# HGRN2 pair products: level 0 and the diagonal by elementwise products and a matrix of ones

## The chip, the cores and the metric

The kernel runs on one core of one Trainium2 chip. The metric is the device time of one execution in microseconds (us). The kernel before took 3584.81 us (median of 3 runs, 3584.51 to 3585.55).

## The reference, cut to what matters

The model is a two-layer backbone over 1024 latent tokens and 256 context tokens of width 1024. Layer 0 (neighbourhood attention beside mLSTM heads) is not touched. Layer 1 has 16 bidirectional HGRN2 heads with 128 keys (k) and 128 values (v). For each head and direction, with `f` the decay after its sigmoid and lower bound, `b` the running sum of `log f`, and `k = 1 - f`, the reference computes in chunks

```python
o = einsum('bhtk,bhkv->bhtv', qc * exp(b), S)
pair = exp(where(tri, b[t] - b[s], -inf))              # t, s in the chunk, for each k
a = einsum('bhtk,bhtsk->bhts', qc, pair * kc)
o = o + einsum('bhts,bhsv->bhtv', a, vc)
S = exp(bL) * S + einsum('bhsk,bhsv->bhkv', kc * exp(bL - b), vc)
```

and adds the outputs of the two directions. `a[t, s]` is a sum over k of a query, a key and the decays between them. Its diagonal is `q[t]·k[t]` without a decay; the entry of a token with its direct neighbour has one decay factor.

## The kernel before, in words

**Layer 1.** `build` loops over 16 heads. For a head, `hg_proj` multiplies the normalised tokens by 128-column slices of the weights: the decay of both directions (`F`, two halves of 512 tokens, and `Fc` for the context) and the query `q` (two halves, half 1 first). `hg_intra` builds the 128x128 score blocks `A` of 8 chunks (4 in each half). `hg_vz` projects values and the output gate, one context tile and then 8 tiles of 128 tokens with 24 matmuls each (`mm<-hh,wzh` and its fellows for the context, `mm<-wzh,hh` for the 8). `hg_ctx` makes the context state, and `hg_scan` runs the states through the 8 chunks (c = 0 to 7), multiplies by `v`, normalises, gates (`gyn`), transposes and stores. `hg_proj` of the next head follows in the program.

**Precision.** A float32 matrix that goes through a projection is split into two float32r parts: `split` (lines 69 to 72) copies the high part on ScalarE (L71) and subtracts it on VectorE (L72). `dense` (L117, L118, L119) then does three float32r matmuls. The matmuls of `hg_level` (L880), the diagonal (L909) and the scan (L920, L932 to L937) are float32. In the profile each float32 128x128 matmul is two MATMUL records and each float32r matmul one; both are labelled f32.

**`hg_intra`, line 834.** For each half: `K = 1 - F` for both directions, `Q = q * F` for both. Then 7 levels, in each of which half 1 goes before half 0. Level `lev` handles the pairs of tokens that first share a block of `2h = 2^(lev+1)` tokens. `hg_level` (line 866) has ScalarE copy the keys of the level to `gksel` (L875), TensorE multiply them by the queries, four 128x128 blocks to a PSUM tile `s` (L880), and VectorE move the entries of this level to `A`: at level 0 by a multiplication with a float32 mask (L886), later by a predicated copy with a byte mask (L890). VectorE then multiplies four half-size slices of K and Q in place by decays (L898) and shrinks the decay products `gT` (L900). At level 0, L888 adds the two directions' keys into another `gksel`; after level 0 `hg_diag` multiplies these by `q` (L909) and L910 writes the diagonal of `A` by a predicated copy.

**What sets the order.** The program is written for the Tile framework with its own scheduler. It orders the instructions of each engine from its own estimate and puts in the semaphores; then each engine goes through its list. The projections of a head and of the next one fill TensorE between the steps of `hg_intra` and `hg_scan`. Buffers that matter here: `gksel` 3, `gsg` 1 (also the sigmoid of `q` in `hg_proj`, L778, read by L779), PSUM `s` 3 and `mm` 2, `gz` 1 (the gate of a head: written by L800, multiplied by L801, read by `gyn`, L953), `gQ`, `gK` and `gA` 2 each, that is one head's two halves. An `mm` tile of `hg_vz` is free for the next but one when VectorE has done L801.

**The end of a scan half.** After chunk 3 and after chunk 7, ScalarE squares four blocks (L948), GpSimd takes the inverse root (L142, L144), VectorE makes four `gyn` (L953), and TensorE transposes them (L956).

Of the kernel before, what the change touches and what calls it, by code (L numbers as in the profile page):

```python
# [18 lines left out]
P = 128  # L19
# [24 lines left out]
class Prog:  # L44
# [789 lines left out]
    def hg_intra(self, st, pool):  # L834
        nc = self.nc
        n = 512
        hv = {}
        for hf in (1, 0):
            F, q = st["F"][hf], st["q"][hf]
            K = self.t(pool, [P, 2, n], F32, "gK", 2)  # L840
            nc.vector.tensor_scalar(out=K, in0=F, scalar1=-1.0, scalar2=1.0, op0=ALU.mult, op1=ALU.add)
            Q = self.t(pool, [P, 2, n], F32, "gQ", 2)
            for d in range(2):
                nc.vector.tensor_tensor(out=Q[:, 1 - d, :], in0=q, in1=F[:, d, :], op=ALU.mult)
            A = self.t(pool, [P, 4, P], F32, "gA", 2)
            hv[hf] = dict(Q=Q, A=A, T=F, K=K)
        for lev in range(7):
            for hf in (1, 0):
                self.hg_level(hv[hf], lev, pool)
            if lev == 0:  # L850
                for hf in (1, 0):
                    self.hg_diag(hv[hf], st["q"][hf], pool)
        for hf in (1, 0):
            H = hv[hf]
            H["kn"] = []
            for d in range(2):
                p = self.ps("tr", [P, 4, P])
                for c in range(4):
                    nc.tensor.transpose(p[:, c, :], H["K"][:, d, c * P : (c + 1) * P], self.ident)
                k_ = self.t(pool, [P, 4, P], F32, "gkn", 4)  # L860
                nc.scalar.copy(k_, p)
                H["kn"].append(k_)
        return hv


    def hg_level(self, H, lev, pool):
        nc = self.nc
        n, h = 512, 1 << lev
        nb = n // (2 * h)
# [6 lines left out]
        qp = pick(Q)  # L876
        pa = self.ps("s", [P, 4, P])
        nbc = P // (2 * h)
        for c in range(4):
            nc.tensor.matmul(  # L880
                pa[:, c, :].rearrange("p (b s i) -> p b s i", s=2, i=h),
                lhsT=ksel[:, c * P : (c + 1) * P], rhs=qp[:, c * nbc : (c + 1) * nbc], start=True, stop=True,
            )
        if lev == 0:

            nc.vector.tensor_tensor(out=A, in0=pa, in1=self.lmask0.unsqueeze(1).to_broadcast([P, 4, P]), op=ALU.mult)  # L886
            H["ks"] = self.t(pool, [P, n], F32, "gksel", 3)
            nc.vector.tensor_tensor(out=H["ks"], in0=K[:, 0, :], in1=K[:, 1, :], op=ALU.add)  # L888
        else:
            nc.vector.copy_predicated(A, self.lmask[:, lev - 1, :].unsqueeze(1).to_broadcast([P, 4, P]), pa)  # L890
        Tv = Tt.rearrange("p d (b s) -> p d b s", s=2)
        bc = lambda t: t.unsqueeze(2).to_broadcast([P, nb, h])
        Kv, Qv = sel(K), sel(Q)
        for t, i, s, tot in (
            (Kv, 0, 0, Tv[:, 0, :, 1]), (Kv, 1, 1, Tv[:, 1, :, 0]),
            (Qv, 0, 0, Tv[:, 1, :, 1]), (Qv, 1, 1, Tv[:, 0, :, 0]),
        ):
            nc.vector.tensor_tensor(out=t[:, i, :, s, :], in0=t[:, i, :, s, :], in1=bc(tot), op=ALU.mult)  # L898
# [5 lines left out]
    def hg_diag(self, H, q, pool):  # L904
        nc = self.nc
        pa = self.ps("s", [P, 4, P])
        for c in range(4):
            s = slice(c * P, (c + 1) * P)
            nc.tensor.matmul(pa[:, c, :], lhsT=H["ks"][:, s], rhs=q[:, s], start=True, stop=True)  # L909
        nc.vector.copy_predicated(H["A"], self.ident8.unsqueeze(1).to_broadcast([P, 4, P]), pa)  # L910

    def hg_scan(self, h, st, halves, S, pool, y):
        nc = self.nc
# [48 lines left out]
    def build(self):  # L962
        tc, nc, a = self.tc, self.nc, self.a
        dma = nc.sync.dma_start
        with ExitStack() as es:
# [19 lines left out]
            def load(name, shape, eng=nc.gpsimd):  # L985
# [12 lines left out]
                out=self.qkn, in0=qkn[:, 0:1], scalar1=qkn[:, 1:2], scalar2=0.125, op0=ALU.mult, op1=ALU.mult  # L998
# [14 lines left out]
            for i in range(2):  # L1013
# [6 lines left out]
                out=self.lb[:, 1, :], in0=self.lb[:, 0, :], scalar1=-1.0, scalar2=1.0, op0=ALU.mult, op1=ALU.add  # L1020
# [74 lines left out]
            lk = l1.enter_context(tc.tile_pool(name="hgk", bufs=1))  # L1095
            with tc.tile_pool(name="op0", bufs=2) as op, ExitStack() as wl:
                self.gate_bc(0, op, 2, 1)
                later = []
                w1 = self.wo_half(wl, a["woab"], 0, "left", yp, later)
                for tt in [8, 9, 3, 4, 2, 5, 1, 6, 0, 7]:  # L1100
                    xt = self.t(op, [P, D], F32, "ox", 2)[:, 512:D]
                    self.out_tile(w2, 1, tt, self.yd, self.xin(tt), xt, yp, op, 2, part=acc[:, tt, :])
                    nc.gpsimd.dma_start(out=self.x1[tt * P : (tt + 1) * P, 512:D], in_=xt)
                    for ld in later[:2]:
                        ld()
                    later = later[2:]
# [5 lines left out]
                nc.vector.tensor_copy(self.ident8, self.ident)  # L1112
                lm = self.t(op, [P, D], F32, "nx", 1)[:, 0 : 7 * P].rearrange("p (l f) -> p l f", f=P)
                dma(out=lm, in_=a["glm"])
                nc.vector.tensor_copy(self.lmask, lm[:, 1:7, :])
                nc.vector.tensor_copy(self.lmask0, lm[:, 0, :])
                self.gate_bc(0, op, 2, 0)
                wr.close()
                right = es.enter_context(ExitStack())
                self.open_h(right)  # L1120
                self.wp = right.enter_context(tc.tile_pool(name="w1", bufs=2, side="right"))
                self.rawp = op
                self.slabs = 4
                wf = self.wring([a["wc"][:, 2048 : 2048 + P]], P)
                for tt in [8, 9, 4, 5, 6, 7, 0, 1, 2, 3]:
                    xt = self.t(op, [P, D], F32, "ox", 2)
                    dma(out=xt[:, 512:D], in_=self.x1[tt * P : (tt + 1) * P, 512:D])
                    self.out_tile(w1, 0, tt, self.yd, self.xin(tt), xt[:, 0:512], op, op, 2)
                    if tt < 8:
                        nc.gpsimd.dma_start(out=self.x1[tt * P : (tt + 1) * P, 0:512], in_=xt[:, 0:512])  # L1130
                    xn = self.t(op, [P, D], F32, "nx", 1)
                    self.norm(xn, xt, op)
                    self.mod_tr(1, [xn], tt, op, self.h_sink(tt * P, P))

            with l1:
                pool = l1.enter_context(tc.tile_pool(name="hg", bufs=2))
                self.rawp = pool
                l1.enter_context(self.pp.phase(s=3, acc=1))
                st = self.hg_proj(0, pool, wf)
                for h in range(16):  # L1140
                    hv = self.hg_intra(st, pool)
# [3 lines left out]
                    if h < 15:  # L1145
                        st = self.hg_proj(h + 1, pool)
# [163 lines left out]
```

## Time and profile before

| what | value |
|---|---|
| median of 3 runs | 3584.81 us |
| the profiled execution, its own time | 3583.22 us |
| span from its first to its last instruction | 3581.4 us |
| mean granted TensorE clock | 0.992 |
| VectorE, ScalarE, GpSimd busy | 2216.1, 1418.4, 454.6 us |
| HGRN2 heads, first to last `gA` mask product | 1948.7 to 3335.4 us |

The busy share of an engine is an average over stages. A line of the timeline has the start, the time from start to end of the merged instructions, the engine, the source line, the operation with its tiles, the count, and in brackets the engine's idle time just before it with what ended it. On TensorE and VectorE one instruction starts before the one ahead of it has quite ended, so a chain's cost is read from start to start. All times are those of the profiled execution.

### The profile page before, as it was taken

The numbers are of one execution on the slowest core, as the hardware profiler recorded it, in microseconds if no ns is written. First come the engines' busy times: TensorE is split into PE (matmuls) and PEld (weight loads), VectorE is DVE, ScalarE is ACT, GpSimd is POOL, SyncE is SP. The second block draws the span as 40 slices with busy tenths as digits, with TensorE's granted clock in tenths as the row PEclk, the third lists the DMA queues.
The fourth block names the chain that finished last, engine by engine and source line by source line (L and its number), as shares of the span: only waits on it lengthen the run. The fifth ranks groups of instructions, "written<-read, shape, count | busy, mean of one in ns | idle before, by whom it ended". The sixth has DMA issues, their size and how long they took to land.

```text
span 3581.4 us, 65599 instructions
## 1 busy us (share of the span) xinstructions
PE 3516.8 (98%) x24954; PEld 3222.6 (90%) x24954; DVE 2216.1 (62%) x5976; ACT 1418.4 (40%) x3493; POOL 454.6 (13%) x752
## 2 busy tenths in 40 slices
PE   8999999999999999998999999999999999999998
PEld 5879999999999999997788999999999999999877
DVE  4646676666754765664666666666666666666653
ACT  5545555445533434433354333333333333333341
POOL 2222222122211212211010000000000000000000
PEclk9999999999999999999999999999999999999999
DMA  5532323232234434324752111111111111110263
GB/s 206 175 103 75 84 70 84 72 89 75 79 96 148 127 93 141 118 72 141 228 158 62 36 36 36 33 36 36 36 35 34 31 36 36 35 33 27 74 205 116
DMA packets 323051, 305.25 MB, mean 85 GB/s; under 512 B 29016, under 2 KB 280088, under 8 KB 322608
## 3 DMA queue, kind: packets, MB, share of 16 engines
q1 hardware_dynamic: 290704, 217.44, 20.9%
q0 software_dynamic: 32032, 83.61, 6.9%
q8 instruction: 197, 3.23, 0.4%
q14 instruction: 118, 0.97, 0.1%
HBM read 241.49 MB, written 59.30 MB: 84 GB/s over the span
## 4 chain that ended last, share of the span: by engine, by line
PE 88%; issue 5%; DMA 3%; DVE 1%; ACT 1%; POOL 1%; SPq 0%; POOLq 0%; DVEq 0%; ACTq 0%
PE mm L119 18%; PE mm L117 18%; PE mm L118 18%; PE s L880 6%; PE mm L729 2%; PE mm L731 2%; PE mm L730 2%; PE acc L674 2%; PE tr L654 2%; PE acc L458 2%; PE s L467 2%; DMA mld<-md 1%; PE acc L448 1%; PE acc L933 1%; PE s L909 1%
## 5 line engine op out<-in xcount | busy, mean ns | idle before, releaser
L119 PE MATMUL mm<-wh,hl 128*128 128x256 f32 x2560 | 748.9, 293 | 0.2 <-DVE hl L250 0.2
L117 PE MATMUL mm<-wh,hh 128*128 128x256 f32 x2560 | 746.5, 292 | 0.0
L118 PE MATMUL mm<-wl,hh 128*128 128x256 f32 x2560 | 745.4, 291 | 0.0
L119 PEld LDWEIGHTS mm<-wh,hl 128*128 128x128 f32 x2560 | 488.5, 191 | 11.1 <-issue 4.1
L117 PEld LDWEIGHTS mm<-wh,hh 128*128 128x128 f32 x2560 | 488.6, 191 | 7.7 <-issue 1.4
L118 PEld LDWEIGHTS mm<-wl,hh 128*128 128x128 f32 x2560 | 488.7, 191 | 7.1 <-issue 0.8
L117 PE MATMUL mm<-hh,wh 128*128 128x512 f32 (+1 forms) x1216 | 449.5, 370 | 5.9 <-ACT gFc L769 5.9
L118 PE MATMUL mm<-hl,wh 128*128 128x512 f32 (+1 forms) x1216 | 449.2, 369 | 0.0
L119 PE MATMUL mm<-hh,wl 128*128 128x512 f32 (+1 forms) x1216 | 448.7, 369 | 0.0
L119 PE MATMUL mm<-wzh,hl 128*128 128x256 f32 x1024 | 295.3, 288 | 0.0
L117 PE MATMUL mm<-wzh,hh 128*128 128x256 f32 x1024 | 294.2, 287 | 0.0
L118 PE MATMUL mm<-wzl,hh 128*128 128x256 f32 x1024 | 293.9, 287 | 0.0
L875 ACT COPY gksel<-gK 128x512 f32<-128x512 f32 x224 | 148.8, 664 | 317.0 <-PE s L880 159.9
L117 PEld LDWEIGHTS mm<-hh,wh 128*128 128x128 f32 x1216 | 230.3, 189 | 37.5 <-ACT gFc L769 6.2
L119 PEld LDWEIGHTS mm<-hh,wl 128*128 128x128 f32 x1216 | 230.3, 189 | 31.7
L118 PEld LDWEIGHTS mm<-hl,wh 128*128 128x128 f32 x1216 | 230.3, 189 | 30.8
L880 PE MATMUL s<-gQ,gksel 128*128 128x128 f32 x1792 | 254.9, 284 | 0.0
L729 PE MATMUL mm<-woh,yh 128*128 128x512 f32 x576 | 229.8, 400 | 5.6 <-DVE oacc L743 3.5
L880 PEld LDWEIGHTS s<-gQ,gksel 128*128 128x128 f32 x1792 | 231.4, 191 | 1.3
L731 PE MATMUL mm<-woh,yl 128*128 128x512 f32 x576 | 229.6, 399 | 0.8 <-DVE yl L72 0.8
L730 PE MATMUL mm<-wol,yh 128*128 128x512 f32 x576 | 229.3, 398 | 0.4 <-DVE wol L72 0.2
L71 ACT CAST wh<-wraw 128x512 fp32r<-128x512 f32 x240 | 147.2, 619 | 202.8 <-PE mm L118 126.2
(307 smaller groups left out, 7349.6 us busy)
## 6 DMA issues: line engine op xcount, KB each, us to landing
wraw<-yd SPq DMA_DIRECT2D x144, 256.0 KB
wraw<-in_wab_dram SPq DMA_DIRECT2D x112, 256.0 KB
md<-ev POOLq DMA_DIRECT2D x100, 256.0 KB, 2.7
wraw<-in_wc_dram SPq DMA_DIRECT2D x96, 256.0 KB
adar<-in_wada_dram POOLq DMA_DIRECT2D x32, 512.0 KB, 4.8
wraw<-in_wc_dram SPq DMA_DIRECT2D x128, 128.0 KB
adar<-in_wada_dram SPq DMA_DIRECT2D x16, 512.0 KB
wraw<-in_wab_dram SPq DMA_DIRECT2D x64, 128.0 KB
```

The source lines that it names most:

```text
L71: nc.scalar.copy(hi, x)
L117: mm(ps, lhsT=lh(k), rhs=rh(k), start=(k == 0), stop=False)
L118: mm(ps, lhsT=lh(k), rhs=rl(k), start=False, stop=False)
L119: mm(ps, lhsT=ll(k), rhs=rh(k), start=False, stop=(k == nk - 1))
L458: nc.tensor.matmul(num, lhsT=qc[:, j, :], rhs=C[d][:, j, :], start=False, stop=(j == 1))
L467: nc.tensor.matmul(u, lhsT=st["k"][c][:, j * P : (j + 1) * P], rhs=vw, start=True, stop=True)
L654: nc.tensor.transpose(pt[:nk, i, :], pr[:, o : o + nk], self.ident)
L729: mm(ps, lhsT=yh[:, k, :], rhs=w.h(kk), start=(kk == 0), stop=False)
L730: mm(ps, lhsT=yh[:, k, :], rhs=w.l(kk), start=False, stop=False)
L731: mm(ps, lhsT=yl[:, k, :], rhs=w.h(kk), start=False, stop=(kk == 8 * len(qs) - 1))
L875: nc.scalar.copy(ksel.rearrange("p (b s i) -> p b s i", s=2, i=h), pick(K))
L880: nc.tensor.matmul(pa[:, c, :].rearrange("p (b s i) -> p b s i", s=2, i=h), lhsT=ksel[:, c * P : (c + 1) * P], rhs=qp[:, c * nbc : (c + 1) ...
```

## The change

Level 0 (a token with its pair neighbour) and the diagonal (a token with itself) no longer go through 128x128 matmuls of keys by queries. A new function `hg_near` runs for both halves before the levels. For each of the two cases it has VectorE multiply keys and queries elementwise into a `gsg` tile `pr` of 128 keys by 512 tokens, splits `pr` into float32r parts (two `gksel` tiles), and has TensorE sum over the 128 keys by two matmuls of a 128x128 matrix of ones with 512 columns. Every row of the result then has the sums, and VectorE keeps the entries wanted: the neighbour by a multiplication with the byte mask of level 0, the diagonal by the predicated copy as before. Level 0 of `hg_level` keeps only the decay multiplications. The float32 mask `lmask0` goes, the byte mask grows by one level, and the ones are built once.

```diff
@@ hg_intra
+        for hf in (1, 0):
+            self.hg_near(hv[hf], st["q"][hf], pool)
         for lev in range(7):
             for hf in (1, 0):
                 self.hg_level(hv[hf], lev, pool)
-            if lev == 0:
-                for hf in (1, 0):
-                    self.hg_diag(hv[hf], st["q"][hf], pool)
@@ hg_level
-        ksel = self.t(pool, [P, n], F32, "gksel", 3)
-        nc.scalar.copy(ksel.rearrange("p (b s i) -> p b s i", s=2, i=h), pick(K))
...
-        if lev == 0:
-
-            nc.vector.tensor_tensor(out=A, in0=pa, in1=self.lmask0.unsqueeze(1).to_broadcast([P, 4, P]), op=ALU.mult)
-            H["ks"] = self.t(pool, [P, n], F32, "gksel", 3)
-            nc.vector.tensor_tensor(out=H["ks"], in0=K[:, 0, :], in1=K[:, 1, :], op=ALU.add)
-        else:
-            nc.vector.copy_predicated(A, self.lmask[:, lev - 1, :].unsqueeze(1).to_broadcast([P, 4, P]), pa)
+        if lev > 0:
+            ksel = self.t(pool, [P, n], F32, "gksel", 3)
+            nc.scalar.copy(ksel.rearrange("p (b s i) -> p b s i", s=2, i=h), pick(K))
...
+            nc.vector.copy_predicated(A, self.lmask[:, lev, :].unsqueeze(1).to_broadcast([P, 4, P]), pa)
@@ hg_diag goes, hg_near comes
-        for c in range(4):
-            s = slice(c * P, (c + 1) * P)
-            nc.tensor.matmul(pa[:, c, :], lhsT=H["ks"][:, s], rhs=q[:, s], start=True, stop=True)
-        nc.vector.copy_predicated(H["A"], self.ident8.unsqueeze(1).to_broadcast([P, 4, P]), pa)
+    def hg_near(self, H, q, pool):
+        nc = self.nc
+        n = 512
+        K, Q, A = H["K"], H["Q"], H["A"]
+
+        kx = bass.AP(K.tensor, K[:, 1, 1:n].offset, [list(K.ap[0]), [2, n // 2], [-(n + 1), 2]])
+        qx = bass.AP(Q.tensor, Q.offset, [list(Q.ap[0]), [2, n // 2], [n + 1, 2]])
+        for i in range(2):
+            hi = self.t(pool, [P, n], F32R, "gksel", 3)
+            lo = self.t(pool, [P, n], F32R, "gksel", 3)
+            pr = self.t(pool, [P, n], F32, "gsg", 1)
+            if i == 0:
+                nc.vector.tensor_tensor(out=pr.rearrange("p (b s) -> p b s", s=2), in0=kx, in1=qx, op=ALU.mult)
+            else:
+                nc.vector.tensor_tensor(out=pr, in0=K[:, 0, :], in1=K[:, 1, :], op=ALU.add)
+                nc.vector.tensor_tensor(out=pr, in0=pr, in1=q, op=ALU.mult)
+            self.split(hi, lo, pr)
+            pa = self.ps("s", [P, 4, P])
+            p2 = pa.rearrange("p a b -> p (a b)")
+            nc.tensor.matmul(p2, lhsT=self.ones, rhs=hi, start=True, stop=False)
+            nc.tensor.matmul(p2, lhsT=self.ones, rhs=lo, start=False, stop=True)
+            if i == 0:
+                nc.vector.tensor_tensor(out=A, in0=pa, in1=self.lmask[:, 0, :].unsqueeze(1).to_broadcast([P, 4, P]), op=ALU.mult)
+            else:
+                nc.vector.copy_predicated(A, self.ident8.unsqueeze(1).to_broadcast([P, 4, P]), pa)
@@ build
-                self.lmask = self.t(lk, [P, 6, P], U8, "glm8", 1)
-                self.lmask0 = self.t(lk, [P, P], F32, "glm0", 1)
+                self.lmask = self.t(lk, [P, 7, P], U8, "glm8", 1)
...
+                self.ones = self.t(lk, [P, P], F32R, "ones", 1)
+                nc.vector.tensor_scalar(
+                    out=self.ones, in0=self.ident, scalar1=0.0, scalar2=1.0, op0=ALU.mult, op1=ALU.add
+                )
...
-                nc.vector.tensor_copy(self.lmask, lm[:, 1:7, :])
-                nc.vector.tensor_copy(self.lmask0, lm[:, 0, :])
+                nc.vector.tensor_copy(self.lmask, lm)
```

More of the change, by code (lines that the diff above doesn't have):

```diff
@@ L873, in hg_level @@
         pick = lambda t: _skew(t[:, 0, :].rearrange("p (b s i) -> p b s i", s=2, i=h), 2, n)
-        ksel = self.t(pool, [P, n], F32, "gksel", 3)
-        nc.scalar.copy(ksel.rearrange("p (b s i) -> p b s i", s=2, i=h), pick(K))
-        qp = pick(Q)
-        pa = self.ps("s", [P, 4, P])
-        nbc = P // (2 * h)
-        for c in range(4):
[L880 to L883, printed above, removed]
-        if lev == 0:
-            nc.vector.tensor_tensor(out=A, in0=pa, in1=self.lmask0.unsqueeze(1).to_broadcast([P, 4, P]), op=ALU.mult)
-            H["ks"] = self.t(pool, [P, n], F32, "gksel", 3)
-            nc.vector.tensor_tensor(out=H["ks"], in0=K[:, 0, :], in1=K[:, 1, :], op=ALU.add)
-        else:
-            nc.vector.copy_predicated(A, self.lmask[:, lev - 1, :].unsqueeze(1).to_broadcast([P, 4, P]), pa)
+        if lev > 0:
+            ksel = self.t(pool, [P, n], F32, "gksel", 3)
+            nc.scalar.copy(ksel.rearrange("p (b s i) -> p b s i", s=2, i=h), pick(K))
+            qp = pick(Q)
+            pa = self.ps("s", [P, 4, P])
+            nbc = P // (2 * h)
+            for c in range(4):
+                nc.tensor.matmul(
+                    pa[:, c, :].rearrange("p (b s i) -> p b s i", s=2, i=h),
+                    lhsT=ksel[:, c * P : (c + 1) * P], rhs=qp[:, c * nbc : (c + 1) * nbc], start=True, stop=True,
+                )
+            nc.vector.copy_predicated(A, self.lmask[:, lev, :].unsqueeze(1).to_broadcast([P, 4, P]), pa)
         Tv = Tt.rearrange("p d (b s) -> p d b s", s=2)
@@ L901, in hg_level @@
         H["T"] = Tn
-    def hg_diag(self, H, q, pool):
+    def hg_near(self, H, q, pool):
         nc = self.nc
-        pa = self.ps("s", [P, 4, P])
-        for c in range(4):
-            s = slice(c * P, (c + 1) * P)
-            nc.tensor.matmul(pa[:, c, :], lhsT=H["ks"][:, s], rhs=q[:, s], start=True, stop=True)
-        nc.vector.copy_predicated(H["A"], self.ident8.unsqueeze(1).to_broadcast([P, 4, P]), pa)
+        n = 512
[12 more added lines that the diff above has]
+            self.split(hi, lo, pr)
+            pa = self.ps("s", [P, 4, P])
+            p2 = pa.rearrange("p a b -> p (a b)")
[5 more added lines that the diff above has]
+                nc.vector.copy_predicated(A, self.ident8.unsqueeze(1).to_broadcast([P, 4, P]), pa)
     def hg_scan(self, h, st, halves, S, pool, y):
@@ L1108, in build @@
                 nc.vector.memset(self.zero, 0.0)
-                self.lmask = self.t(lk, [P, 6, P], U8, "glm8", 1)
-                self.lmask0 = self.t(lk, [P, P], F32, "glm0", 1)
+                self.lmask = self.t(lk, [P, 7, P], U8, "glm8", 1)
                 self.ident8 = self.t(lk, [P, P], U8, "ident8", 1)
                 nc.vector.tensor_copy(self.ident8, self.ident)
+                self.ones = self.t(lk, [P, P], F32R, "ones", 1)
+                nc.vector.tensor_scalar(
+                    out=self.ones, in0=self.ident, scalar1=0.0, scalar2=1.0, op0=ALU.mult, op1=ALU.add
+                )
                 lm = self.t(op, [P, D], F32, "nx", 1)[:, 0 : 7 * P].rearrange("p (l f) -> p l f", f=P)
                 dma(out=lm, in_=a["glm"])
-                nc.vector.tensor_copy(self.lmask, lm[:, 1:7, :])
-                nc.vector.tensor_copy(self.lmask0, lm[:, 0, :])
+                nc.vector.tensor_copy(self.lmask, lm)
                 self.gate_bc(0, op, 2, 0)
```

## The prediction

> **What bounds the kernel now.** I read the page first, then busy time by stage, then the timelines of the engines in one head. The page's first lines, and the windows of two heads one after the other (length, then busy time and instructions of TensorE, weight load, VectorE, ScalarE, GpSimd, then the clock):
>
> ```profile
> span 3581.4 us, 65599 instructions
> PE 3516.8 (98%) x24954; PEld 3222.6 (90%) x24954; DVE 2216.1 (62%) x5976; ACT 1418.4 (40%) x3493; POOL 454.6 (13%) x752
> 2592.90:2685.10 92.20, 92.20 (x652) 86.08 (x651) 60.36 (x150) 29.95 (x74) 4.27 (x6) 1.00 0.12 35
> 2685.10:2777.30 92.20, 92.20 (x652) 86.07 (x651) 60.19 (x150) 29.74 (x74) 4.27 (x6) 1.00 0.12 35
> ```
>
> The same counts in windows of 92.20 us: a head takes 92.2 us. TensorE never shows idle at the full clock, VectorE is busy 65%. A modelled end can hide a gap, so I go by starts. TensorE around the end of a head's query projection:
>
> ```profile
> 2682.15 0.39 PE L117 MATMUL mm<-hh,wh 128*128 128x512 f32 x1
> 2682.38 0.39 PE L118 MATMUL mm<-hl,wh 128*128 128x512 f32 x1
> 2682.84 1.16 PE L880 MATMUL s<-gQ,gksel 128*128 128x128 f32 x6
> 2683.83 0.39 PE L934 MATMUL acc<-gS,gQ 128*128 128x128 f32 x2
> 2684.06 0.39 PE L932 MATMUL acc<-gv,gA 128*128 128x128 f32 x2
> 2684.51 0.39 PE L934 MATMUL acc<-gS,gQ 128*128 128x128 f32 x2
> 2691.18 0.61 PE L909 MATMUL s<-gq,gksel 128*128 128x128 f32 x4
> 2691.63 0.38 PE L956 MATMUL tr<-ident,gyn 128*128 128x128 f32 x2
> 2624.03 0.28 PE L117 MATMUL mm<-wzh,hh 128*128 128x256 f32 x1
> 2624.15 0.28 PE L118 MATMUL mm<-wzl,hh 128*128 128x256 f32 x1
> ```
>
> Start to start: a float32r matmul of 512 columns 0.23 us, of 256 columns 0.12 us; a float32 128x128 matmul, two records, 0.225 us (four L909 records in 0.45 us). Level 0 stands out: six L880 records in 0.99 us, so 0.33 us a matmul. Its moving operand alternates between the two directions' queries. So TensorE sets the end of this stage: what leaves it is gained, unless it then has to wait.
>
> **The change part by part.** *TensorE.* Removed in a head: 8 level-0 matmuls x 0.33 = 2.64 us and 8 of the diagonal x 0.225 = 1.80 us. Added: 8 of ones x 0.23 = 1.84 us. That is 2.6 us a head and 41.6 us in 16 heads, without waits. The Trainium skill, page "FP8 and Floating Point Precision", section "TensorE Precision Notes", says that true FP32 takes four passes through the array. By this a 128-column float32 matmul costs as much as one of 512 columns in one pass, at every level; the rows of the diagonal agree (0.225 against 0.23), those of level 0 do not, and by the rule the gain without waits would be 8 x 0.225 x 16, some 29 us.
>
> *VectorE and ScalarE.* A half gains four VectorE instructions of 512 columns: the neighbour product, the product by `q`, and two low parts. (The sum of the keys and the two writes to `A` were there.) ScalarE has two casts in place of one copy. VectorE's price, start to start, stands in this timeline of before around the same place:
>
> ```profile
> 2683.46 0.69 DVE L72 TENSOR_TENSOR wl<-wraw,wh 128x512 fp32r<-128x512 f32 x1 [2.39 <-ACT wh L71]
> 2684.07 0.68 DVE L779 TENSOR_TENSOR gq<-gsg,mm 128x512 f32<-128x512 f32 x1
> 2685.26 0.69 DVE L886 TENSOR_TENSOR gA<-s,glm 128x512 f32<-128x512 f32 x1 [0.51 <-PE s L880]
> 2685.87 0.42 DVE L898 TENSOR_TENSOR gQ<-gQ,gF 128x256 f32<-128x256 f32 x1
> 2688.41 0.61 DVE L953 SCALAR_TENSOR_TENSOR gyn<-acc,gss,gz 128x128 f32<-128x128 f32 x2
> 2688.94 0.75 DVE L898 TENSOR_TENSOR gK<-gK,gF 128x256 f32<-128x256 f32 x2
> 2691.39 0.69 DVE L886 TENSOR_TENSOR gA<-s,glm 128x512 f32<-128x512 f32 x1 [1.70 <-PE s L880]
> 2693.85 0.73 DVE L910 COPY_PREDICATED gA<-ident,s 128x512 f32<-128x512 uint8 x1
> 2694.47 0.41 DVE L815 TENSOR_SCALAR gq<-gFc 128x512 f32<-128x512 f32 x1
> 2694.80 0.75 DVE L898 TENSOR_TENSOR gK<-gK,gT 128x256 f32<-128x256 f32 x2
> 2695.47 0.74 DVE L910 COPY_PREDICATED gA<-ident,s 128x512 f32<-128x512 uint8 x1
> 2696.76 0.28 DVE L801 TENSOR_TENSOR gz<-gz,mm 128x128 f32<-128x128 f32 x1
> 2696.96 0.72 DVE L890 COPY_PREDICATED gA<-glm,s 128x512 f32<-128x512 uint8 x1
> ```
>
> So 0.61 us for 512 columns, 0.62 for a predicated copy, 0.67 for a pair of half-size products, 0.53 for a pair of `gyn`. Eight new instructions are 4.9 us a head. From 2693 on VectorE runs without a gap, so in this stretch it has no room for them. The product reads at a skewed step that no row shows on VectorE: at least the 0.61, at most twice that, by the factor 1.5 of level 0's matmul rounded up; I take 0.61 and keep 1.2 for the range.
>
> *Order.* Each engine goes through its list in order, so I laid the changed kernel's lists beside these prices, with zero at the end of the second query projection (2682.84 in before). In the changed kernel TensorE has the gate and value tiles and the scan of chunks 4 to 7 there; the last scan matmul (chunk 7) stands at 8.2, where before has it at 1.7. The four sums stand at about 7, 10 to 11, 13 and 17, and the third gate tile at 13.45, if nothing waits. That tile needs a PSUM buffer that VectorE's first L801 frees. Behind chunk 7 comes a chain of which before shows each link:
>
> ```profile
> 2684.99 0.28 ACT L948 ACTIVATE gjk<-acc 128x128 f32<-128x128 f32 x1 [1.07 <-PE acc L934]
> 2686.66 0.28 POOL L142 TENSOR_SCALAR gss<-gss 128x4 f32<-128x4 f32 x1 [5.90 <-ACT gjk L948]
> 2687.02 1.36 POOL L144 TENSOR_TENSOR gss<-gss,mhalf 128x4 f32<-128x4 f32 x1
> 2668.55 1.03 POOL L144 TENSOR_TENSOR gss<-gss,mhalf 128x4 f32<-128x4 f32 x1
> 2694.71 0.28 ACT L800 ACTIVATE gz<-mm 128x128 f32<-128x128 f32 x1
> 2699.20 0.27 ACT L799 COPY gv<-mm 128x128 f32<-128x128 f32 x1 [0.39 <-PE mm L119]
> ```
>
> From chunk 7's matmul (2684.51) to `gyn` (2688.41) is 3.9 us; one value copy now stands between the squares (2694.71 less its start, some 0.16 us), so `gyn` starts at 8.2 + 4.1 = 12.3. Behind it in VectorE's list, ahead of L801, the odd heads have two `gyn`, the diagonal's copy, two half-size products, the low part of the third sum, two `gyn`, the sum of the keys and the mask product: 0.53 + 0.62 + 0.67 + 0.61 + 0.53 + 0.61 + 0.61 = 4.2. L801 starts at 16.5 and its 0.28 is over at 16.75; TensorE, there since 13.45, waits 3.3 us. In the even heads the copy and the products stand ahead of `gyn`, 2.9 us remain, L801 is over at 15.5, and the wait is 2.05 us. Both heads run into the low part of the third sum on the way; that wait lies inside these. In before L801 was done at 2697.04, and the second gate tile only ended at 2699.2, so the third had 2 us to spare.
>
> The first four heads and the last have lists of their own. The same steps give 0.5, 6.2 (chunk 7 stands at 13.0 there), 2.0, 2.8 and 2.3 us. With six even heads at 2.05 and five odd at 3.3 the waits are 13.8 + 12.3 + 16.5 = 42.6 us. After the wait the levels are paced by TensorE again: it comes to level 2 about 1 to 2 us after VectorE has the queries ready. Edits that I cost at nothing: ScalarE's casts (ScalarE is busy 30 of 92 us, and the casts are done 1 to 4 us ahead of their matmuls), and ones and masks, built once.
>
> *Sum.* 41.6 less 42.6 us: 1 us slower; where GpSimd's root takes 1.03 and not 1.36 us, as in the other scan half of before, the odd heads have 0.3 us less, 1.6 us in all. I call it nothing: 3583 us, against the 3583.2 us of the profiled execution. The median of the runs lies 1.6 us over that. The Trainium skill, page "SBUF — State Buffer", section "Who interferes with whom", says that a VectorE instruction with two SBUF inputs contends with a GpSimd instruction that reads SBUF. The two lengths of L144 would fit it. By it the even heads, where VectorE is busy during the root, keep 1.36 and the odd ones, where it waits for the root, get 1.03; that is the 1.6 us above.
>
> **The rivals.** *The cover holds* (faster): TensorE has other work or L801 comes sooner, and most of the 41.6 us stays. All of it gives 3541, half of the wait 3562. For it speaks that before has no wait in this stage; against it, that TensorE's list is fixed, and that eight links must all be shorter than their rows. A VectorE chain shorter by 0.5 us gives 8 us, 3575.
>
> *Weight splits ahead of the levels* (slower): in the changed list VectorE's splits of the next head's gate weights stand ahead of the last two levels and of the context's scan (L813, L814). Before has them after:
>
> ```profile
> 2634.46 0.68 DVE L813 TENSOR_TENSOR_SCAN gEc<-gFc,gzero 128x255 f32<-128x255 f32 x1 [1.54 <-issue]
> 2636.42 0.68 DVE L72 TENSOR_TENSOR wzl<-wraw,wzh 128x512 fp32r<-128x512 f32 x1
> 2639.90 0.62 ACT L71 CAST wzh<-wraw 128x512 fp32r<-128x512 f32 x1 [1.50 <-DMA wraw<-in_wc_dram]
> 2640.55 0.69 DVE L72 TENSOR_TENSOR wzl<-wraw,wzh 128x512 fp32r<-128x512 f32 x1 [1.71 <-ACT wzh L71]
> 2644.27 0.62 ACT L71 CAST wzh<-wraw 128x512 fp32r<-128x512 f32 x1 [3.27 <-DMA wraw<-in_wc_dram]
> ```
>
> Each piece waits for a load that starts when the one ahead is split: 2.8 to 3.0 us from split to cast. Three pieces then end about 51.3 in the head, L814 at 52.6, and the context's decay leaves its buffer at 53.1, which TensorE wants at 53.8. It is 0.6 us to spare; beyond it each 1 us of a later load costs 1 us a head. At 1.5 us later it is 0.9 x 16 = 14 us: 3597. A skewed product at 1.2 us costs the even heads up to 0.5 us, 4 us in all.
>
> *The sums are not cheap* (the change does not do what it says): a matmul of ones whose operand was just split starts late. At 0.31 instead of 0.23 each, 128 of them cost 10 us more: 3593.
>
> **How the numbers follow.** A measurement of this kernel can tell about 0.2% from no change, 7 us. The forecast, saving and wait within 7 us of each other, has 0.44; the cover 0.29 (0.10 of it below 3556); the weight splits 0.21; the dear sums 0.06. So faster 0.29, same 0.44, slower 0.27. The likeliest case's own range is 3576 to 3590. The range of 3556 to 3606 takes in waits of up to 1.7 us a head fewer or 1.4 us more than the 2.7 us reckoned, and leaves out 0.1 at each end.
>
> **What would show it.** Right: a steady head of 91 to 93 us; L880 at six sevenths of its count; about 128 ones matmuls at 0.23 us; TensorE idle of 2 to 3 us a head ahead of the third gate tile (L117, `mm<-wzh,hh`) put down to VectorE's `gz`; busy share near 97%. Wrong: a head of 89.6 us and no idle; or idle ahead of L769's tiles, put down to ScalarE (the weight splits), or ahead of the levels' L880; or L144 or the product far from the lengths taken.

## The result, and the profile after

The changed kernel takes 3604.04 us (median of 6 runs, 3600.99 to 3608.99) against 3584.66 us of the kernel before in runs beside it (6 runs, 3583.67 to 3586.78): ratio 1.0055, 95% interval 1.0042 to 1.0068. It is slower by 19 us: inside the range of the prediction, but the forecast was no change. The profiled execution is the slowest of the six, 3608.99 us.

The page of the changed kernel: the span, the engines' busy time, the gate tiles' group, and the group of the output projections, of which the one behind the heads holds the 6.4 us (last column: idle time of TensorE just before, and what ended most of it).

```profile
span 3606.9 us, 64896 instructions
PE 3509.7 (97%) x24570; PEld 3192.6 (89%) x24570; DVE 2299.0 (64%) x6104; ACT 1430.6 (40%) x3525; POOL 451.9 (13%) x752
L117 PE MATMUL mm<-wzh,hh 128*128 128x256 f32 x1024 | 301.0, 294 | 15.7 <-DVE gz L801 15.7
L729 PE MATMUL mm<-woh,yh 128*128 128x512 f32 x576 | 231.3, 402 | 10.6 <-ACT yh L71 6.4
```

TensorE is busy 7 us less than before, yet the span is 25.5 us longer: the time went into waits and into stretches at a lower clock, both shown below. Heads measured from one second query projection to the next, in windows of the changed kernel (length, busy time of TensorE, weight load, VectorE, ScalarE, GpSimd, then the granted clock): the second head, one of those with a lower clock, an even one, an odd one. (Even and odd go by the program's count from 0; "the second head" and the like count from one. So the eighth and the tenth head are odd ones.)

```profile
2036.20:2135.70 99.50, 95.49 (x633) 87.40 (x632) 67.77 (x163) 32.66 (x84) 6.34 (x8) 0.95 0.10 30
2789.30:2884.10 94.80, 92.33 (x627) 85.06 (x626) 65.56 (x158) 30.49 (x75) 4.15 (x6) 0.98 0.11 34
2884.10:2976.20 92.10, 90.68 (x627) 83.61 (x626) 65.36 (x158) 30.69 (x76) 3.94 (x6) 1.00 0.12 36
2976.20:3069.50 93.30, 90.83 (x627) 83.57 (x626) 65.56 (x158) 30.58 (x76) 4.14 (x6) 1.00 0.11 34
```

Before, a head took 92.2 us at a clock of 1.00. Of the 25.5 us, the fifteen lengths from the first head's second query projection to the last one's hold 17.0 (1399.0 against 1382.0 us); 4.2 lie ahead of them, where the change only builds the ones and the masks, and 4.3 behind them.

The odd head in the timeline, TensorE first, then VectorE:

```profile
2988.98 0.49 PE L969 MATMUL tr<-ident,gyn 128*128 128x128 f32 x2
2989.23 0.48 PE L918 MATMUL s<-gksel,ones 128*128 128x512 f32 x1
2991.02 0.50 PE L919 MATMUL s<-gksel,ones 128*128 128x512 f32 x1 [1.31 <-DVE gksel L72]
2991.36 0.51 PE L969 MATMUL tr<-ident,gyn 128*128 128x128 f32 x2
2993.03 0.36 PE L117 MATMUL mm<-wzh,hh 128*128 128x256 f32 x1 [1.15 <-DVE gz L801]
```

```profile
2986.71 0.84 DVE L911 TENSOR_TENSOR gsg<-gK,gQ 128x512 f32<-128x512 f32 x1
2988.49 0.61 DVE L966 SCALAR_TENSOR_TENSOR gyn<-acc,gss,gz 128x128 f32<-128x128 f32 x2 [0.94 <-POOL gss L144]
2989.01 0.72 DVE L923 COPY_PREDICATED gA<-ident,s 128x512 f32<-128x512 uint8 x1
2989.62 0.75 DVE L892 TENSOR_TENSOR gQ<-gQ,gF 128x256 f32<-128x256 f32 x2
2990.29 0.68 DVE L72 TENSOR_TENSOR gksel<-gsg,gksel 128x512 fp32r<-128x512 f32 x1
2990.89 0.60 DVE L966 SCALAR_TENSOR_TENSOR gyn<-acc,gss,gz 128x128 f32<-128x128 f32 x2
2991.41 0.68 DVE L913 TENSOR_TENSOR gsg<-gK 128x512 f32<-128x512 f32 x1
2992.01 0.68 DVE L921 TENSOR_TENSOR gA<-s,glm 128x512 f32<-128x512 f32 x1
2992.61 0.47 DVE L801 TENSOR_TENSOR gz<-gz,mm 128x128 f32<-128x128 f32 x2
```

From L918 to L919 lie 1.79 us from start to start where 0.23 would do, and from the last transpose (2991.55 in the records, 0.19 after the pair's start) to the gate tile 1.48 where 0.11 would do: 1.56 and 1.37 us. With 0.11 lost behind L919 itself (0.34 to the next start) that is 3.04 us. VectorE goes without a gap from `gyn` to L801, and both waits of TensorE end in this one queue. The even head has the same with less ahead of the low part:

```profile
2896.99 0.45 PE L969 MATMUL tr<-ident,gyn 128*128 128x128 f32 x2
2897.70 0.50 PE L919 MATMUL s<-gksel,ones 128*128 128x512 f32 x1 [0.27 <-DVE gksel L72]
2898.03 0.51 PE L969 MATMUL tr<-ident,gyn 128*128 128x128 f32 x2
2899.70 0.36 PE L117 MATMUL mm<-wzh,hh 128*128 128x256 f32 x1 [1.16 <-DVE gz L801]
```

Here it is, in order of time, 0.49 + 0.11 + 1.37 = 1.97 us. One thing isn't in the prediction at all. Windows around the same wait in the head that took 94.8 us, the clock third from the end:

```profile
2802.30:2806.20 3.90, 1.43 (x7) 0.76 (x6) 3.90 (x11) 1.21 (x4) 0.18 (x1) 1.00 0.00 0
2806.50:2810.00 3.50, 3.50 (x20) 3.50 (x19) 2.35 (x6) 1.21 (x2) 0.12 (x1) 0.53 0.23 80
2810.00:2814.00 4.00, 4.00 (x33) 3.91 (x32) 2.55 (x7) 2.18 (x5) 0.00 (x0) 0.98 0.00 0
```

TensorE ran 1.43 of 3.9 us, and for the next 3.41 us its granted clock is half: 20 matmuls start in 3.5 us where 33 start in the 4.0 us behind. The trace has six such stretches inside the heads, each 15 to 18 us behind a second query projection, that is right behind these waits; five last 3.41 us, the one in the second head 10.24. Before has none inside a head. A steady odd head with one takes 94.8 to 95.2 us in place of 93.3. The Trainium skill, page "TensorE: Matmul & The Clock Gate", section "Part 1: The HAM clock gate (the "warmup" mystery)", has the clock at half or full by the activity in a free-running window of 3413 ns; the length of the stretches agrees. Its section "HAM oscillation — how this bites in real kernels" gives as the rule to have no gaps over some 3.4 us. That is not enough here: the longest single wait of a steady head was 1.6 us. Its section "A second HAM failure mode: psum-queue depth-cycling", by which frequent short idle times are enough to swing the clock, is the one that comes nearest; no run here shows the mechanism.

### The profile page after: what moved, and what is told of

The parts are those of the page before. It is cut to its first block, busy times and chain, and to the rows that moved or that the text cites. A ratio compares the mean times of both kernels' runs of the same rounds, so it can differ in the third digit from the quotient of the medians.

```text
span 3606.9 us, 64896 instructions
## 1 busy us (share of the span) xinstructions
PE 3509.7 (97%) x24570; PEld 3192.6 (89%) x24570; DVE 2299.0 (64%) x6104; ACT 1430.6 (40%) x3525; POOL 451.9 (13%) x752
## 4 chain that ended last, share of the span: by engine, by line
PE 83%; issue 6%; DMA 4%; DVE 3%; ACT 1%; POOL 1%; SPq 0%; POOLq 0%; DVEq 0%; ACTq 0%
PE mm L117 17%; PE mm L119 17%; PE mm L118 17%; PE s L880 5%; PE acc L674 2%; PE mm L729 2%; PE mm L731 2%; PE mm L730 2%; PE tr L654 2%; PE s L467 2%; PE acc L458 2%; PE acc L448 1%; PE acc L946 1%; PE acc L947 1%; PE acc L945 1%
## 5 line engine op out<-in xcount | busy, mean ns | idle before, releaser
L117 PE MATMUL mm<-wzh,hh 128*128 128x256 f32 x1024 | 301.0, 294 | 15.7 <-DVE gz L801 15.7
L72 DVE TENSOR_TENSOR wl<-wraw,wh 128x512 fp32r<-128x512 f32 x240 | 163.9, 688 | 131.3 <-ACT wh L71 125.6
L117 PEld LDWEIGHTS mm<-wzh,hh 128*128 128x128 f32 x1024 | 198.4, 194 | 19.1 <-issue 17.1
L880 PE MATMUL s<-gQ,gksel 128*128 128x128 f32 x1536 | 205.4, 276 | 0.0
```

The lines of the kernel that those rows point to most:

```text
L72: nc.vector.tensor_tensor(out=lo, in0=x, in1=hi.bitcast(F32), op=ALU.subtract)
L117: mm(ps, lhsT=lh(k), rhs=rh(k), start=(k == 0), stop=False)
L880: nc.tensor.matmul(pa[:, c, :].rearrange("p (b s i) -> p b s i", s=2, i=h), lhsT=ksel[:, c * P : (c + 1) * P], rhs=qp[:, c * nbc : (c + 1) ...
```

## The experiments

The theory: TensorE's waits are set by where its fixed list puts a matmul against where VectorE's fixed list puts what frees it; the waits, and the half clock behind them, eat the saving. Rivals: eight more VectorE instructions cost by themselves wherever they stand; the sums by ones are not cheaper on TensorE. The medians of the kernel before beside these runs are 3584.9 to 3586.3 us.

**One part alone: the neighbour's product.** The own-token product is back on the matmul, as before.

```diff
@@ hg_near
-        for i in range(2):
+        for i in range(1):
@@ hg_intra, hg_level: hg_diag and H["ks"] are back
```

> Only the neighbour product by ones; the diagonal stays a float32 matmul. Theory (the waits come from where the third gate tile stands in TensorE's list against VectorE's L801): TensorE saves 8 x 0.33 - 4 x 0.23 = 1.7 us a head; the tile stands at 14.6 us of the head instead of 13.5, and only one low part and one product come new into VectorE's list, so the wait falls to 1 us or less: 3565 to 3580. Rival (VectorE has too much to do, each new instruction costs its length): half of the eight instructions cost half of the loss of 37 us a head sum, 3594. Rival (the ones matmuls are dear): 3575.

Measured: 3567.22 us (3563.28 to 3568.64), ratio 0.9946 (0.9932 to 0.9961): inside the theory's range, and faster than both kernels. Every steady head takes 90.94 us, no head holds half clock, and TensorE shows no idle time in a steady one (window of one head):

```profile
2674.90:2765.80 90.90, 90.90 (x640) 84.46 (x639) 62.89 (x154) 29.96 (x74) 4.22 (x6) 1.00 0.12 36
```

This part of the change by itself is a gain.

**One part alone: the own token.** Level 0 stays on the matmul; the diagonal goes by ones (`gS1` has 8 buffers instead of 10 to make room).

```diff
@@ hg_intra, against the kernel before; hg_near makes only K[:,0]+K[:,1], times q, split, two matmuls
             for hf in (1, 0):
+                if lev == 0:
+                    self.hg_near(hv[hf], st["q"][hf], pool)
                 self.hg_level(hv[hf], lev, pool)
@@ hg_diag keeps only the predicated copy of these sums, after level 0
```

> Only the diagonal by ones; level 0 stays a float32 matmul. Theory: TensorE saves 8 x 0.225 - 4 x 0.23 = 0.9 us a head; the third gate tile moves between 11 and 18 us from head to head, so the waits are 0 to 3 us: 3575 to 3600. Rival (VectorE has too much to do): half the loss, 3594, in even heads and odd ones alike.

Measured: 3602.64 us (3597.8 to 3604.78), ratio 1.0049 (1.0032 to 1.0066), 2.6 us over the theory's range. From one second query projection to the next it takes 89.2 and 96.7 us in turn, mostly because the order puts more matmuls into one than into the other (660 against 620). A pair of heads takes 185.9 us, where before has 184.4. The wait is not the one that the theory named: the third gate tile has 1.3 us in all, and the first line is another one (us in total, times, longest):

```profile
PE s L882 <- DVE gQ L898: 10.4, 13, 1.7
```

Both parts add four VectorE instructions to a head, and they are 35 us apart. By the savings expected of them (1.7 and 0.9 us a head) 13 of the 35 us are TensorE's own work. VectorE's load by itself does not explain the rest. That the place where its queue is met explains it is not shown by these two, since their orders and the buffers of `gS1` differ too; the next runs try it with the same work.

**The two waits, one by one.** In the changed kernel both products go through the one `gsg` buffer, which also holds the sigmoid of `q`. `gknc`, the buffer of the context's keys, is free at that point. First the neighbour's product goes there:

```diff
-            pr = self.t(pool, [P, n], F32, "gsg", 1)
+            pr = self.t(pool, [P, n], F32, "gsg" if i else "gknc", 1)
```

> Same work on every engine as the changed kernel; only the neighbours' product goes into another buffer (the one of the normalized keys, free at that point) than the own-token product, so that a half's products no longer wait for a buffer that the half before still reads. In the order of TensorE this puts the third gate tile 15.5 us behind the second q projection instead of 13.5. Theory (TensorE waits for the gate multiplication behind VectorE's queue, and the clock halves after such waits): the 2.0 and 3.1 us of waits in a head and the half clock go, a head is 92.2 less 2.3 us of TensorE saving, about 90 us against 93.3 on average in the changed kernel, so 3604 less 16 times 3.2: 3550 to 3570, unless another wait shows on the page. Rival, VectorE's eight more instructions cost by themselves wherever they stand: 3598 to 3608. Rival, the sums by ones aren't cheaper on TensorE than the products they replace: 3590 to 3606.

Then the other way round (`"gknc" if i else "gsg"`), and both in `gknc`:

> As the kernel with the neighbours' product in the buffer of the normalized keys (3569 us), but with the buffers swapped: the own-token product in that buffer, the neighbours' product in the one of the sigmoid of q. The third gate tile stands at 15.5 us here too, the first sums at 6.2 us instead of 3.1. Theory (the place of the third gate tile against the 15.5 us at which its PSUM tile is free decides): no wait there, 3562 to 3578. Rival (what counted was that the neighbours' product no longer waits for the sigmoid's buffer): 3595 to 3606, as that wait is back.

> Both products in the buffer of the normalized keys, none in the sigmoid's. The first sums go to 1.4 to 3.2 us, and the third gate tile stands at 13.2 to 13.5 us, as in the changed kernel. Theory (the place of the third gate tile decides): it waits about 2 us in each head as in the changed kernel, heads of 92 us or more, 3590 to 3612. Rival (what counted was that the products no longer wait for the sigmoid's buffer): 3562 to 3580.

Measured: 3569.3 us (3568.0 to 3571.9; ratio 0.9956, 0.9941 to 0.9971), 3599.07 us (3595.13 to 3600.18; 1.0033, 1.002 to 1.0046) and 3629.15 us (3625.22 to 3629.83; 1.0117, 1.01 to 1.0134). The counts of instructions on every engine are the same in all of them. The waits of TensorE, over the whole span: the changed kernel, the first, the swapped and the one-buffer kernel.

```profile
PE mm L117 <- DVE gz L801: 15.7, 14, 1.2
PE s L919 <- DVE gksel L72: 9.3, 13, 1.3
```

```profile
PE s L919 <- DVE gksel L72: 4.3, 16, 0.3
PE s L880 <- ACT gksel L875: 2.9, 15, 0.3
```

```profile
PE s L919 <- DVE gksel L72: 20.4, 29, 1.4
```

```profile
PE mm L117 <- DVE gz L801: 16.2, 14, 1.2
PE mm L117 <- ACT gFc L769: 10.1, 7, 5.9
PE tr L969 <- DVE gyn L966: 7.4, 15, 0.6
```

The places of the third gate tile are counted in TensorE's list without waits; in the traces it starts later, at 16.9 us in the first kernel, at 18.2 in the swapped one, at 16.1 to 16.4 in the one-buffer kernel and at 15.6 and 16.8 in the changed one. Where it stands at 15.5 us (first and swapped) its wait is gone, where it stands at 13.2 to 13.5 it is there: the theory's place. The first kernel is inside the theory's range, though its heads take 91.2 us and not 90. The swapped kernel missed the theory's number, and 3599 us is in the rival's range: it keeps the other wait, 1.2 and 0.3 us in each head on two low parts, and its heads take 92.5 us. In its trace VectorE loses the time earlier, waiting for TensorE to have read an older `gksel`:

```profile
2509.68 0.69 DVE L72 TENSOR_TENSOR gksel<-gknc,gksel 128x512 fp32r<-128x512 f32 x1 [1.18 <-PE s L918]
```

Its first sums start at 6.1 us, those of the first kernel at 3.0. The changed kernel goes the same way: at 7.3 us in the odd heads, with a wait of 1.56 us on the low part, and at 5.9 in the even ones, with 0.49. That the place of the first sums sets this wait fits all of them; it was not tried by itself. So there are two waits, each with a condition of its own, and the changed kernel has both. In the one-buffer kernel the wait at the third gate tile is there as expected, and its rival falls, but it is 17 us over the theory's range: it has other waits, and 11 of its 15 heads hold a stretch of half clock. With the first kernel both of its rivals fall: the same VectorE instructions and the same sums, 35 us less.

**Less work.** The low parts are left out (one matmul for a sum, no subtraction).

```diff
-            self.split(hi, lo, pr)
+            nc.scalar.copy(hi, pr)
...
-            nc.tensor.matmul(p2, lhsT=self.ones, rhs=hi, start=True, stop=False)
-            nc.tensor.matmul(p2, lhsT=self.ones, rhs=lo, start=False, stop=True)
+            nc.tensor.matmul(p2, lhsT=self.ones, rhs=hi, start=True, stop=True)
```

> Leaves out the low parts: one matmul of ones for a sum, and no subtraction on VectorE (the split is one copy on ScalarE), so it is less work on both engines. TensorE has 4 matmuls fewer in a head (0.92 us, 15 us in all), VectorE 4 instructions fewer (about 2.6 us). The third gate tile stands at 14.6 us. Theory of the waits: with 1.1 us more ahead of the third tile and 1.3 us or more off VectorE's queue the wait of 2 us is gone, and the clock stays up: 3604 less 16 times 3.2 less 15, 3540 to 3565. Rival, VectorE's load by itself: half of the 20 us come back, and TensorE's 15: 3575 to 3582. Rival, it is only the TensorE work of the sums: 3587 to 3591.

Measured: 3566.43 us (3565.11 to 3570.46), ratio 0.9949 (0.9934 to 0.9964), a little over the theory's range: heads of 90.76 us. It does less than the first buffer kernel and is only 3 us faster; 9.1 us of a new wait (L917, for ScalarE's copy) took most of the rest.

**The neighbour alone, with the free buffer** (`"gknc"` for its product):

> The neighbour-only kernel (own-token product back on the matmul as before), with the product in the buffer of the normalized keys. Its first sums stand 3.1 us behind the second q projection and its third gate tile 16.4 us. Theory of the waits: the neighbour-only kernel had hardly any wait of TensorE left (period 90.9 us), so it gives the same within 5 us, 3560 to 3570, unless the earlier sums now wait for their products (then up to 1.5 us a head more, 3590). Rival, a shorter VectorE queue is worth something everywhere: the work is the same, so 3567.

Measured: 3579.41 us (3577.2 to 3582.39), ratio 0.9982 (0.9973 to 0.9991): a miss by 9 us. Steady heads take 91.75 us, 0.8 more than with `gsg`; from start to start 0.4 us more go behind the transposes and 0.6 behind level 1. The free buffer is no gain by itself: it gives another order, and that order has waits of its own.

**Taking the third tile's wait away by a copy.** ScalarE copies the raw gate out of PSUM, so that the `mm` tile is free without VectorE; the control does the same to the kernel before.

```diff
-            nc.vector.tensor_tensor(out=z[:, tt, :], in0=z[:, tt, :], in1=ps[:, P:256], op=ALU.mult)
+            zr = self.t(pool, [P, P], F32, "gzr", 2)
+            nc.scalar.copy(zr, ps[:, P:256])
+            nc.vector.tensor_tensor(out=z[:, tt, :], in0=z[:, tt, :], in1=zr, op=ALU.mult)
@@ gS1: 8 buffers instead of 10
```

> The change whole, but ScalarE copies the gate's raw values out of PSUM (two small buffers), so that the mm tile no longer waits for VectorE's L801; eight copies of about 0.17 us more for ScalarE in a head, and gS1 has 8 buffers instead of 10. Theory: the wait ahead of the third gate tile (1.4 us in each head) goes, that at the third sum (0.1 or 1.6 us) stays, and few stretches at half clock are left: 3570 to 3585. Rival (VectorE has too much to do): the wait turns up at the levels or the fourth sum, 3600 to 3610.

> The kernel before with the raw gate copied out of its PSUM tile by ScalarE and multiplied from SBUF, and eight buffers of gS1 instead of ten: the control of the same edit on the changed kernel, which gave 3630. Theory: in the kernel before no wait of TensorE hangs on the gate, so the edit changes only ScalarE's load by 16 copies a head and the order: 3580 to 3595. If it gives 3605 or more, the copy or the fewer buffers themselves cost the 25 us, and not what the copy did to the order of the changed kernel.

Measured: 3629.99 us (3624.95 to 3631.74), ratio 1.0121 (1.0106 to 1.0136), a clear miss, over the rival's range too; the control 3588.68 us (3583.06 to 3591.38), ratio 1.0006 (0.9997 to 1.0016), as expected, with eight copies a head and not 16. The copy has no measurable cost where nothing hangs on it. In the changed kernel the wait is gone and the next one is longer:

```profile
PE tr L971 <- DVE gyn L968: 25.8, 11, 2.6
PE s L921 <- DVE gksel L72: 10.9, 14, 1.1
PE mm L117 <- ACT gF L769: 6.1, 10, 1.7
```

Eleven of the fifteen heads hold half clock.

**Filling the idle time.** Six useless matmuls of ones ahead of the third sum; then, in another kernel, twelve useless repeats of the last transpose, just ahead of the third gate tile.

```diff
+            for r in range(0 if i else rep - 1):
+                nc.tensor.matmul(p2, lhsT=self.ones, rhs=hi, start=True, stop=True)
```

> The change whole, and six useless matmuls of ones (0.23 us each, 1.4 us a head, 22 us in all) ahead of the third sum's own, so that TensorE works where it would wait. Theory: they fall into the waits and cost nothing, and no stretch at half clock is left inside the heads: 3588 to 3604, with less spread between runs. Rival (TensorE's own work still sets the head): 3626. Rival (the clock has no part): 3604 to 3612, with the same spread.

```diff
-                nc.tensor.transpose(pt[:, i, :], yn, self.ident)
+                for r in range(13 if c == 7 and i == 3 else 1):
+                    nc.tensor.transpose(pt[:, i, :], yn, self.ident)
```

> The changed kernel with the last of the eight transposes of a head's normalized output issued 13 times instead of once (useless work, same result), so that TensorE works while the third gate tile waits for the gate multiplication: 12 more of 0.11 us, 1.3 us in the 1.37 us of that wait, 21 us of added work in all. In the order of TensorE everything else keeps its place; the third tile goes from 13.5 to 14.8 us and the wait should fall to 0.1 us, while odd heads keep their 1.6 us ahead of the second matmul of the first sum. Theory (the waits stay what they are, the half clock after them costs the rest): even heads stay at 92.1 us and odd ones at 93.3, but TensorE is idle for 1.7 us at most in one place, so the stretches of half clock go from the heads, and with them about 1.5 us for each of the five of the profiled execution and about 5 in the second head: 3588 to 3597. Rival, the half clock has nothing to do with the waits or costs nothing: 3602 to 3606. Rival, TensorE's work is the bound here and every added instruction counts: 3620 to 3626.

Measured: 3608.7 us (3603.53 to 3613.64; ratio 1.0064, 1.0049 to 1.0079) and 3602.52 us (3599.78 to 3607.23; 1.005, 1.0038 to 1.0063). Some 20 us of useless TensorE work cost 5 us and nothing: TensorE's work was not the bound in this stretch. But both times are in the range of the rival for which the clock has no part or costs nothing, and not in the theory's. In the first kernel four heads still hold half clock, where none was expected: the waits on the low part and at the third gate tile are all but gone, and others stand in their place (9.0 us for ScalarE's cast ahead of the sums).

In the second kernel half clock is left only in the second head, as the theory said, but the time stayed. Its order did not: in the odd heads the first sums stand at 5.9 us instead of 7.3, and with the wait at the third gate tile that on the low part is gone too. The odd heads are shorter for it, 92.5 to 92.8 us after 93.3, and the even ones longer, 93.5 to 95.3 after 92.1. Windows of an even and of an odd head, then lines of its waits:

```profile
2885.40:2979.50 94.10, 92.59 (x642) 84.99 (x641) 66.56 (x160) 30.55 (x76) 4.24 (x6) 1.00 0.12 35
2979.50:3072.00 92.50, 91.73 (x638) 84.48 (x637) 64.90 (x156) 30.82 (x76) 3.74 (x6) 1.00 0.12 35
PE mm L117 <- ACT gFc L769: 10.6, 8, 5.9
PE s L918 <- ACT gksel L71: 4.3, 8, 2.9
PE tr L970 <- DVE gyn L966: 3.5, 7, 0.5
```

The `gFc` wait is 4.7 us longer in all than in the changed kernel's first profile, and the new ones lie in the even heads, 40 us behind the third gate tile: the delay was passed on, not removed. So the runs did not price the half clock by taking it away; its price is from heads of one kernel, with and without it.

**The changed kernel again.**

> The changed kernel once more, for a second profile of it. Theory: periods of the heads without half clock are the same as in the first profile (92.1 even, 93.3 odd), and those with it longer by 1.5 us; which heads have it may change, and the time goes with their number: 3599 to 3609 with four to eight stretches inside the heads, the 4 us that the first profile lost ahead of the heads may be missing. Rival, the half clock belongs to certain heads by the program: the same heads have it, and the time of a profiled run is 3608 again.

Measured: 3605.72 us (3602.4 to 3606.92), ratio 1.0056 (1.0043 to 1.007); span of the profiled run 3604.0. Steady even heads take 92.1, odd ones 93.3 without half clock and 94.8 to 95.7 with it. L801's wait is again 15.7 us in 14 times. Four of the five heads with half clock are the same ones as in the first profile; the third and the eighth head have lost it (93.6 and 93.4 in place of 94.8 and 94.9), the sixth has got it (94.8 in place of 93.4). So it comes and goes with the execution: neither the theory's count alone nor the rival's fixed heads. Only 1.4 us are lost ahead of the heads here, so at least 2.8 of the 4.2 us of the first profile were chance; behind the last head it is 6.8.

## Why the prediction was wrong

- **The bound** was right: TensorE's list in the heads, and a wait of it is lost.
- **The order and the waits** were right to 0.3 us. Odd head: `gyn` foretold 12.3 us behind the second query projection, in the trace at 12.3 (2988.49); L801 16.5, at 16.4; the instructions between in the foretold order; wait 3.3, measured 3.04. Even head: 2.05 and 1.97. The first four heads were further off: 0.5, 6.2, 2.0 and 2.8 us were foretold, and the trace shows none, 3.9, 1.4 and 2.0 us of waits in that stretch. In the second and the fourth the longest (2.9 and 1.5) is for ScalarE's cast of a product, ahead of its sum; the prediction put the casts at nothing.
- **The saving on TensorE** was too large: an even head less its waits is 92.1 - 1.97 = 90.1 us, so 2.1 us are saved and not 2.6. From start to start over a whole head the removed matmuls were 2.5 and 1.7 us, the ones take 1.96 and not 1.84. That is up to 0.5 x 16 = 8 us of the miss. The term of level 0 (2.64) and that of the diagonal (1.80) were each 0.1 too large, that of the ones 0.12 too small.
- **The failing step** is the sum, "41.6 less 42.6 us", in which saving and waits cancel. The saving was 2.1 us a head and not 2.6, and a wait was priced at its own length. Behind the waits TensorE ran 3.41 us at half clock in five heads of the first profile (about 1.5 us each, 7.5; the eighth head took 94.85 us with it and 93.35 without it in two executions of the same kernel) and 10.24 us in the second head. There the wait was foretold at 6.2 us and the page of its window shows 2.9 + 0.7 + 0.3; the half clock made up for it (99.5 us measured, 94.5 - 2.6 + 6.2 = 98.1 foretold). Over the fifteen lengths the forecast is 1382.0 - 15 x 2.6 + 40.3 = 1383.3 us and 1399.0 were measured, 15.7 more. The smaller saving (7.5), the half clock of five heads (7.5) and the second head (1.4) are 16.4 us, so they account for it to about 1 us.
- **Behind the heads**: 4.3 and 6.8 us more than before in the two profiles. The page has a wait of the output projection for ScalarE's `yh` there, 6.4 and 6.5 us, foretold nowhere; in before the same matmuls wait 1.9 us there. The neighbour kernel with the free buffer has 5.1 of it too, the faster buffer kernel 2.2. What brings it about was not tried and stays open.
- **The skewed product** is between the bounds: 0.84 us in its record where plain ones have 0.68, so about 0.16 more.
- **GpSimd's root** came out the other way round: the sentence drawn from the Trainium skill gave the even heads 1.36 and the odd ones 1.03 us. Measured, even and odd:

```profile
2895.09 1.03 POOL L144 TENSOR_TENSOR gss<-gss,mhalf 128x4 f32<-128x4 f32 x1
2986.91 1.54 POOL L144 TENSOR_TENSOR gss<-gss,mhalf 128x4 f32<-128x4 f32 x1
```

In the odd heads the skewed product (L911, two SBUF inputs) runs for the first half of the root; in the even ones the predicated copy, whose one input is PSUM, takes most of it. This agrees in its direction with the rule of the Trainium skill, page "SBUF — State Buffer", section "Who interferes with whom"; what was wrong was which instruction would stand there. Not every row follows it: in the even heads a product with two SBUF inputs (L892) runs beside the last 0.3 us of the root, which still takes 1.03.

- **The rivals**: the cover (3562 for half the wait) is what the first buffer kernel shows (3569), by one buffer that the change did not use. The weight splits hardly showed: no wait for `gFc` in the heads of the changed kernel's first profile, two of 1.0 us together in the heads of the second. Dear sums: 0.12 us a head, 2 us in all.

What stays open: why one head goes to half clock after 3 us of waits and another does not, and by how much the half clock alone makes the kernel longer.

## What to carry to other kernels

Add up what a change takes from the bounding engine, and then walk its list against the list of the engine that feeds it: here the choice of a buffer for one product decided 35 us with the same work. When a wait is taken away or filled, ask for the next in the queue before counting the gain; such an edit also moves the rest of the order. Of the six edits here that kept the change whole and moved, filled or took away a wait, one gained more than 6 us. Price 2 to 3 us of waits on TensorE at more than their length, since the clock may fall for some us behind them: here one such stretch cost about 1.5 us.

## What the runs showed of the hardware

TensorE's granted clock fell to half for 3.41 us behind two waits of 1.56 and 1.37 us within 4.5 us, though neither lasted 2 us by itself; in the swapped kernel waits of 1.34 to 1.36 and of 0.49 us within 3 us did it in two heads, and of 1.68 and 0.49 us in a third. Other heads with the same waits kept the full clock. Matmuls of 256 columns start 0.21 us apart in such a stretch instead of 0.12.
